# A seven-product (Strassen) block form for the input projection of one hybrid encoder layer

## The chip, the cores and the metric

One core of a Trainium2 chip runs the whole layer in one launch. The metric is the device time of an execution in microseconds, the median of several runs. Its engines are TensorE (PE for its matmuls, PEld for its weight loads), VectorE (DVE), ScalarE (ACT), GpSimd (POOL) and the queue that issues DMAs (SP).

## The reference

One layer, sequence 1024, model width 1024, all in float32:

```python
proj = x @ w_in + b_in                    # [1024, 1024] @ [1024, 8192]
a_u, a_v, a_g, b_z, b_g, c_val, c_glu, c_g, merge, ple_g = split(proj)   # 512 each; merge 3072, ple_g 1024
y_a = gelu(a_u) * spatial_mix(layer_norm(gelu(a_v))) * silu(a_g)
y_b = real(fft2(b_z)) * silu(b_g)
y_c = silu(group_norm(conv31(c_val * sigmoid(c_glu)))) * silu(c_g)
merged = sum(sigmoid(merge[b]) * (y[b] @ w_p[b]) for b in (a, b, c))
out = layer_norm(alpha * x + merged @ w_out + b_out + sigmoid(ple_g) * (p @ w_ple))
```

The input projection is the bulk: 64 output tiles of 128 channels.

## The kernel before, in words

Every float32 operand of a matmul is held as two parts, hi (rounded, a cast on ScalarE) and lo (the rest, a subtraction on VectorE; both in `split`, lines 79 to 81), and each product takes three matmuls: hi with hi, hi with lo, lo with hi. All matmuls that matter have a 128 x 128 stationary operand and 512 moving columns.

x stays in SBUF transposed and split, eight k tiles of 128 rows (`xs`). The projection is walked in units. A channel-major unit (`t_unit`, line 228) computes 128 channels for 1024 positions: 8 k x 3 x 2 halves = 48 matmuls into two PSUM banks, and then an activation or a product takes the banks away. A position-major pass (`natural_pass`, line 145) computes 512 channels with the positions on the partitions: 8 k x 8 position tiles x 3 = 192 matmuls into eight banks; there are four, for b_z, a_v and the two halves of ple_g. Weights come in tiles of 128 x 1024 (512 KB) by `load_split` (line 88): a raw tile by a DMA on SP's queue, then the split; three buffers each of raw, hi and lo, and the whole is put 300 instructions ahead of its place.

The order is written out by hand: b_z, the transform with b's gates, branch B's merges, the spatial gating, branch A's merges with the convolution's normalisation in steps between them, branch C, the embedding product with ple_g, and the output projection with the layer norm. A merge (`merge_pair`, line 325) computes its sigmoid gate by a unit and multiplies it at once with y @ w_p; nothing is written to DRAM but the result. The convolution's 31 taps are 1024-wide VectorE operations (`tap`, line 382) taken from a list, `bgq`, some after each unit. Each engine works its instructions off in order. The tile framework orders them by priority when it builds the program, assigns buffers, and sets the waits for data, for buffers and for banks.

Of the kernel before, what the change touches and what calls it, by code (L numbers as in the profile page):

```python
# [9 lines left out]
F32 = mybir.dt.float32  # L10
# [13 lines left out]
HALF = 512  # L24
AHEAD4 = 60
AHEAD = 300  # instructions by which a weight's split goes ahead of the arithmetic
# [6 lines left out]
R_BZ, R_AV, R_AG, R_AB, R_PG, R_BO, R_LG, R_LB = 0, 512, 1024, 1536, 2048, 3072, 4096, 5120  # L33


@with_exitstack
def hybrid_layer(
# [22 lines left out]
    rows = ctx.enter_context(tc.tile_pool(name="rows", bufs=1))  # L60
    s2 = ctx.enter_context(tc.tile_pool(name="s2", bufs=7))
    xp = ctx.enter_context(tc.tile_pool(name="xp", bufs=16))
    s4 = ctx.enter_context(tc.tile_pool(name="s4", bufs=21))
    st = ctx.enter_context(tc.tile_pool(name="st", bufs=8))
    psp = ctx.enter_context(tc.tile_pool(name="psp", bufs=8, space=bass.MemoryType.PSUM))
# [4 lines left out]
    def slot(shape, dt=F32, name="t4"):  # L70
        return s4.tile([P, *shape], dt, name=name, tag="s4")

    def xslot(name):
        return xp.tile([P, 1024], F32R, name=name, tag="xp")

    def tmp(dt=F32, name="t2"):
        return s2.tile([P, HALF], dt, name=name, tag="s2")

# [4 lines left out]
    def load(src):  # L83
        raw = wraw.tile([P, 1024], F32, name="raw", tag="raw")
        nc.sync.dma_start(out=raw, in_=src)
        return raw

    def load_split(src):
        with tc.high_priority(AHEAD):
            raw = load(src)  # L90
            hi = whi.tile([P, 1024], F32R, name="hi", tag="hi")
            lo = wlo.tile([P, 1024], F32R, name="lo", tag="lo")
            split(hi, lo, raw)
        return hi, lo

    def load_split4(src):
        with tc.high_priority(AHEAD4):
            raw = load(src)
            hi, lo = slot([1024], F32R, "h4"), slot([1024], F32R, "l4")
            split(hi, lo, raw)  # L100
        return hi, lo
# [6 lines left out]
    def row_tile():  # L108
        return rows.tile([P, 1024], F32, name="row", tag="row")

    def mm3(ps, s, m, first, last):
        (sh, sl), (mh, ml) = s, m
        nc.tensor.matmul(ps, lhsT=sh, rhs=mh, start=first, stop=False)  # L113
        nc.tensor.matmul(ps, lhsT=sh, rhs=ml, start=False, stop=False)  # L114
        nc.tensor.matmul(ps, lhsT=sl, rhs=mh, start=False, stop=last)  # L115
# [4 lines left out]
    # ---------------- b_z, in position-major form; x arrives meanwhile  # L120
    xs = []
    col = const.tile([P, C_END], F32, name="col")
# [10 lines left out]
    bsT = const.tile([P, 4, P], F32, name="bsT")  # L133

    def load_x(kt, parts):
        raw = wraw.tile([P, 1024], F32, name="raw", tag="raw")
        hi, lo = xslot("xh"), xslot("xl")
        xs.append((hi, lo))
        n = 1024 // parts
        return [  # L140
            (raw[:, i * n:(i + 1) * n], xT[kt][:, i * n:(i + 1) * n], hi[:, i * n:(i + 1) * n], lo[:, i * n:(i + 1) * n])
            for i in range(parts)
        ]

    def natural_pass(unit, evac, ns=range(NPT), before=None, after=None):
        banks = {n: bank() for n in ns}
        w = None
        for kt in range(KT):
            if before is not None:
                w = before(kt, w)  # L150
            elif kt % 2 == 0:
                w = load_split(w_in[unit + kt // 2])
            wk = sub(w, slice(None), slice((kt % 2) * HALF, (kt % 2 + 1) * HALF))
            for n in ns:
                mm3(banks[n], sub(xs[kt], slice(None), slice(n * P, (n + 1) * P)), wk, kt == 0, kt == KT - 1)
            if after is not None:
                after(kt)
        for n in ns:
            evac(n, banks[n])

    def x_arrives(kt, w):
        if kt == 0:
            raw = wraw.tile([P, 1024], F32, name="raw", tag="raw")
            hi = whi.tile([P, 1024], F32R, name="hi", tag="hi")
            lo = wlo.tile([P, 1024], F32R, name="lo", tag="lo")
            pieces = load_x(0, 2)
            wp = [(raw[:, i * HALF:(i + 1) * HALF], w_in[BZ][:, i * HALF:(i + 1) * HALF],
                   hi[:, i * HALF:(i + 1) * HALF], lo[:, i * HALF:(i + 1) * HALF]) for i in range(2)]
            for r, src, h, l in (wp[0], pieces[0], pieces[1], wp[1]):
                nc.sync.dma_start(out=r, in_=src)  # L170
                split(h, l, r)
            return hi, lo
        for r, src, h, l in load_x(kt, 1):
            nc.sync.dma_start(out=r, in_=src)
            split(h, l, r)
        if kt % 2 == 0:
            w = load_split(w_in[BZ + kt // 2])
        if kt >= KT - 3:
            tab.append(load_split4(tabs[kt - KT + 3]))
        if kt == 1:  # L180
            nc.sync.dma_start(out=col, in_=colp)
            x_arrives.bz = row(tmp(name="row"), R_BZ)
        return w

    tab = []
    zj = [slot([2, HALF], F32, "z") for _ in range(4)]

    def evac_z(n, ps):
        nc.vector.tensor_tensor(out=zj[n // 2][:, n % 2], in0=ps, in1=x_arrives.bz, op=ALU.add)

    natural_pass(BZ, evac_z, before=x_arrives)

    for i in range(2):
        nc.vector.tensor_copy(out=cen[:, i], in_=tab[2][0][:, 768 + i * P:768 + (i + 1) * P].bitcast(F32))
# [6 lines left out]
    def add(o, a, b):  # L201
        nc.vector.tensor_tensor(out=o, in0=a, in1=b, op=ALU.add)

    def subt(o, a, b):
        nc.vector.tensor_tensor(out=o, in0=a, in1=b, op=ALU.subtract)

    def mul(o, a, b):
        nc.vector.tensor_tensor(out=o, in0=a, in1=b, op=ALU.mult)

    s02, s13 = slot([2, HALF], F32, "s02"), slot([2, HALF], F32, "s13")  # L210
    add(s02, zj[0], zj[2])
    subt(zj[0], zj[0], zj[2])
    add(s13, zj[1], zj[3])
    subt(zj[1], zj[1], zj[3])
    add(zj[2], s02, s13)
    subt(zj[3], s02, s13)

    # ---------------- channel-major unit: 128 channels of the projection
    bgq = []

    pace = [0]

    def bg():
        """Some of the instructions that wait to be mixed in."""
        for _ in range(min(pace[0], len(bgq))):
            bgq.pop(0)()

    def t_unit(ct, evac):
        w = load_split(w_in[ct])
        banks = [bank() for _ in range(2)]  # L230
        (wh, wl) = w
        for kt in range(KT):
            ks = slice(kt * P, (kt + 1) * P)
            xh, xl = xs[kt]
            for wt, xt, f, l in ((wh, xh, True, False), (wh, xl, False, False), (wl, xh, False, True)):
                for hf in range(2):
                    nc.tensor.matmul(  # L237
                        banks[hf], lhsT=wt[:, ks], rhs=xt[:, hf * HALF:(hf + 1) * HALF],
                        start=f and kt == 0, stop=l and kt == KT - 1,
                    )  # L240
        for hf in range(2):
            evac(hf, banks[hf])
        bg()

    def act_unit(ct, func, dst):
        def evac(hf, ps):
            nc.scalar.activation(out=dst(hf), in_=ps, func=func, bias=col[:, ct:ct + 1])
        t_unit(ct, evac)

    # ---------------- Fourier mixing  # L250
    gT = [None] * 4
# [4 lines left out]
    def split_group(g):  # L256
        gs = slice(g * P, (g + 1) * P)
        fh, fl = slot([4, 2, P], F32R, "fh"), slot([4, 2, P], F32R, "fl")
        for k in range(4):
            split(fh[:, k], fl[:, k], zj[k][:, :, gs])  # L260
        F[g] = (fh, fl)
# [63 lines left out]
    def merge_pair(branch, y, d2, step=None):  # L325
        wp = load_split(w_p[branch * 4 + d2])
        for i in range(2):
            d = 2 * d2 + i
            if branch == 1:
                merged[d] = slot([1024], F32, "mg")  # L330
# [421 lines left out]
```

## Time and profile before

| | us |
|---|---|
| three runs | 995.39, 995.79, 995.84 |
| median | 995.79 |
| span of the profiled execution | 994.7 |
| TensorE busy | 984.7 (4420 matmuls) |
| VectorE busy | 569.7 |
| ScalarE busy | 294.5 |
| GpSimd busy | 21.2 |
| DMA, mean over the span | 67 GB/s |

Busy time is time with at least one instruction in the engine; matmuls overlap, so a matmul's price is read from the distance between starts in the chain. The granted clock is given as a share of TensorE's full 2.4 GHz; it was 0.999 in the mean.

### The profile page before, as it was taken

What the parts mean: (1) busy time and instruction counts of PE and PEld (TensorE: products, weight loads), DVE (VectorE), ACT (ScalarE), POOL (GpSimd) and SP (SyncE); (2) the same over time, 40 slices, a digit from 0 to 9 for tenths busy, and PEclk for the clock granted to TensorE, in tenths of its full rate; (3) what the DMA queues carried; (4) which work ended last, traced back from release to release, by engine and by line L of the source; (5) the groups of instructions that cost most, each with busy time, mean ns of one, the idle gap of its engine ahead of it and who ended that gap; (6) DMA issues with size and microseconds to landing.
All of it is one profiled execution on the core that took longest, in us unless ns stands there. A gap on an engine that the chain in (4) does not pass through costs nothing.

```text
span 994.7 us, 10596 instructions
## 1 busy us (share of the span) xinstructions
PE 984.7 (99%) x4420; PEld 814.6 (82%) x4420; DVE 569.7 (57%) x684; ACT 294.5 (30%) x424; POOL 21.2 (2%) x20
## 2 busy tenths in 40 slices
PE   9999999999999999999999999999999999999997
PEld 6888888888888888888888888888887888888886
DVE  4553369818979976973445646433231311757587
ACT  4333322121211345233336455332211230333100
POOL 0000000000000210000000000000000000000022
PEclk9999999999999999999999999999999999999999
DMA  8611101111121231111111111111221110232312
GB/s 253 216 43 43 33 31 43 43 64 43 43 74 48 102 106 43 43 46 61 43 43 43 43 64 36 50 43 49 78 64 43 57 60 32 70 112 95 128 64 105
DMA packets 20751, 67.10 MB, mean 67 GB/s; under 512 B 2272, under 2 KB 3168, under 8 KB 20704
## 3 DMA queue, kind: packets, MB, share of 16 engines
q1 hardware_dynamic: 20704, 66.43, 19.8%
q8 instruction: 34, 0.56, 0.2%
q14 instruction: 13, 0.11, 0.0%
HBM read 62.23 MB, written 4.19 MB: 67 GB/s over the span
## 4 chain that ended last, share of the span: by engine, by line
PE 98%; DMA 1%; DVE 0%; ACT 0%; SPq 0%; POOLq 0%; issue 0%
PE ps L237 53%; PE ps L341 13%; PE ps L115 11%; PE ps L114 10%; PE ps L113 10%; DMA raw<-in_xT_dram 1%; PE ps L536 0%; PE ps L537 0%; PE ps L548 0%; PE ps L549 0%; SPq L170 0%; DVE zacc L445 0%; DVE xl L81 0%; ACT xh L80 0%; ACT hi L80 0%; POOLq L748 0%
## 5 line engine op out<-in xcount | busy, mean ns | idle before, releaser
L81 DVE TENSOR_TENSOR lo<-raw,hi 128x1024 fp32r<-128x1024 f32 (+1 forms) x88 | 106.2, 1207 | 236.6 <-ACT hi L80 236.4
L237 PE MATMUL ps<-xh,hi 128*128 128x512 f32 x768 | 236.9, 390 | 0.7 <-ACT hi L80 0.7
L237 PE MATMUL ps<-xl,hi 128*128 128x512 f32 x768 | 236.6, 389 | 0.0
L237 PE MATMUL ps<-xh,lo 128*128 128x512 f32 x768 | 236.5, 389 | 0.0
L80 ACT CAST hi<-raw 128x1024 fp32r<-128x1024 f32 (+1 forms) x88 | 91.9, 1044 | 485.8 <-PE ps L237 341.9
L237 PEld LDWEIGHTS ps<-xh,lo 128*128 128x128 f32 x768 | 144.2, 188 | 30.1
L237 PEld LDWEIGHTS ps<-xl,hi 128*128 128x128 f32 x768 | 144.1, 188 | 30.1
L237 PEld LDWEIGHTS ps<-xh,hi 128*128 128x128 f32 x768 | 143.6, 188 | 30.3 <-ACT hi L80 1.1
L389 DVE SCALAR_TENSOR_TENSOR acc<-h,col,acc 128x1009 f32<-128x1009 f32 (+14 forms) x120 | 153.1, 1276 | 3.3
L113 PE MATMUL ps<-hi,xh 128*128 128x512 f32 x256 | 100.1, 391 | 0.2 <-ACT xh L80 0.2
L115 PE MATMUL ps<-hi,xl 128*128 128x512 f32 x256 | 99.6, 390 | 0.5 <-DVE xl L81 0.5
L114 PE MATMUL ps<-lo,xh 128*128 128x512 f32 x256 | 99.6, 389 | 0.0
L341 PE MATMUL ps<-yh,hi 128*128 128x512 f32 x192 | 59.1, 389 | 0.0
L341 PE MATMUL ps<-yh,lo 128*128 128x512 f32 x192 | 59.1, 389 | 0.0
L341 PE MATMUL ps<-yl,hi 128*128 128x512 f32 x192 | 59.1, 389 | 0.0
L113 PEld LDWEIGHTS ps<-hi,xh 128*128 128x128 f32 x256 | 48.2, 188 | 11.4 <-ACT xh L80 1.4
L115 PEld LDWEIGHTS ps<-hi,xl 128*128 128x128 f32 x256 | 48.0, 188 | 11.0 <-DVE xl L81 1.0
L114 PEld LDWEIGHTS ps<-lo,xh 128*128 128x128 f32 x256 | 48.2, 188 | 9.9
L341 PEld LDWEIGHTS ps<-yh,hi 128*128 128x128 f32 x192 | 36.0, 188 | 7.5
L341 PEld LDWEIGHTS ps<-yl,hi 128*128 128x128 f32 x192 | 36.0, 188 | 7.5
L341 PEld LDWEIGHTS ps<-yh,lo 128*128 128x128 f32 x192 | 36.0, 188 | 7.5
L439 POOL TENSOR_TENSOR rstd<-var,mhalf 128x1 f32<-128x1 f32 x16 | 21.0, 1316 | 968.3 <-DVE var L437 968.3
(134 smaller groups left out, 967.9 us busy)
## 6 DMA issues: line engine op xcount, KB each, us to landing
raw<-in_w_in_dram SPq DMA_DIRECT2D x67, 512.0 KB, 3.3
raw<-in_w_p_dram SPq DMA_DIRECT2D x12, 512.0 KB, 3.2
raw<-in_x_dram SPq DMA_DIRECT2D x16, 256.0 KB, 2.7
raw<-in_w_out_dram SPq DMA_DIRECT2D x8, 512.0 KB, 3.6
raw<-in_xT_dram SPq DMA_DIRECT2D x7, 512.0 KB, 4.9
out_dram<-zacc SPq DMA_DIRECT2D x7, 512.0 KB, 2.6
row<-in_rowp_dram SPq DMA_DIRECT2D x5, 512.0 KB, 5.6
raw<-in_tabs_dram SPq DMA_DIRECT2D x3, 512.0 KB, 3.3
```

Of the source, the lines that this page charges most:

```text
L80: nc.scalar.copy(out=hi, in_=src)
L81: nc.vector.tensor_tensor(out=lo, in0=src, in1=hi.bitcast(F32), op=ALU.subtract)
L113: nc.tensor.matmul(ps, lhsT=sh, rhs=mh, start=first, stop=False)
L114: nc.tensor.matmul(ps, lhsT=sh, rhs=ml, start=False, stop=False)
L115: nc.tensor.matmul(ps, lhsT=sl, rhs=mh, start=False, stop=last)
L237: nc.tensor.matmul(banks[hf], lhsT=wt[:, ks], rhs=xt[:, hf * HALF:(hf + 1) * HALF], start=f and kt == 0, stop=l and kt == KT - 1,)
L341: nc.tensor.matmul(banks[hf], lhsT=wp[wi][:, ws], rhs=y[k][hf][yi], start=f and k == 0, stop=l and k == 3,)
L389: nc.vector.scalar_tensor_tensor(out=acc[i][:, a:b], in0=h[:, a + o:b + o], scalar=w, in1=acc[i][:, a:b], op0=ALU.mult, op1=ALU.add)
L439: nc.gpsimd.tensor_tensor(out=r2, in0=r, in1=mhalf, op=ALU.pow)
```

## The change

The projection is computed in blocks. x is cut into 2 x 2 blocks by halves of the model width and of the positions, and the weights by halves of the width and by two neighbouring units (or two neighbouring 512-channel passes). Seven products of blocks, P1 to P7, give what eight gave. The seven x sides are blocks or sums of blocks, made once and split, and stay in SBUF in place of x (`quad_first`, `quad_rest`). The weight sides that are sums are made by DMAs on GpSimd's queue that add a block of DRAM to the raw tile that holds the previous sum (`plus`). P6 and P7 are added in PSUM to the bank x of P1, P4 and P3 to the banks x and z; copies of the bank are taken in between (`keep`, `kept`).

Units go in pairs (24 of them), two pairs interleaved: P1 of the pair, P7 of the pair before, P2, P4 and P3 of the pair before, P5, P6. A product has 12 matmuls in one bank, and one background step (a mixing tile, a tap, a step of the convolution's normalisation) follows each. The two position-major units (b_z with a_v, the two halves of ple_g) have 4 k x 4 position tiles x 3 matmuls in each product.

Since the x sides fill SBUF, results are not kept: gates, z, v, mixed values, y and the residual are stored to DRAM (`store`) and loaded again. The order becomes: embedding product, b_z with a_v, ple_g, the pairs, then the merges of A, C and B with the transform's steps between them, and the output projection. Raw, hi and lo tiles become 128 x 512, with 9, 6 and 6 buffers; temporary tiles go from 7 to 12.

```diff
-    wraw = ctx.enter_context(tc.tile_pool(name="wraw", bufs=3))
-    whi = ctx.enter_context(tc.tile_pool(name="whi", bufs=3))
-    wlo = ctx.enter_context(tc.tile_pool(name="wlo", bufs=3))
+    rawp = ctx.enter_context(tc.tile_pool(name="rawp", bufs=9))
+    hip = ctx.enter_context(tc.tile_pool(name="hip", bufs=6))
+    lop = ctx.enter_context(tc.tile_pool(name="lop", bufs=6))
...
+    def plus(dst, src):
+        nc.gpsimd.dma_start(out=dst, in_=src, accum_op=ALU.add)
...
+        def product(p, banks, first):            # natural_unit: position-major
+            ws = sides(p)
+            for k in range(4):
+                between(p, k)
+                for n in range(4):
+                    xs = sub(X[p][k], slice(None), slice(n * P, (n + 1) * P))
+                    mm3(banks[n], xs, ws[k], first and k == 0, k == 3, not first)
...
+        product(P6, bx, False)
+        kept("u2", (row1, 1))
+        product(P7, bx, False)
+        kept("u3", (row2, -1))
...
+    def quad_rest(k):
+        b11, b12 = x_block(k, 0, 0), x_block(k, 0, 1)
+        t1 = rawt()
+        subt(t1, b11, b12)
+        split(*X[P5][k], t1)
+        b22 = x_block(k, 1, 1)
+        split(*X[P3][k], b22)
+        subt(b12, b22, b12)
+        split(*X[P7][k], b12)
+        t2 = b11
+        nc.vector.scalar_tensor_tensor(out=t2, in0=t1, scalar=-1.0, in1=b22, op0=ALU.mult, op1=ALU.subtract)
+        split(*X[P6][k], t2)
+        b21 = x_block(k, 1, 0)
+        t4 = t1
+        nc.vector.scalar_tensor_tensor(out=t4, in0=t2, scalar=-1.0, in1=b21, op0=ALU.mult, op1=ALU.subtract)
+        split(*X[P4][k], t4)
...
+        def side(self, p):                       # Pair: channel-major
+            with tc.high_priority(AHEAD):
+                if p == P1:
+                    self.a11, self.a12 = load(self.block(0, 0)), load(self.block(0, 1))
+                    self.a21, self.a22 = load(self.block(1, 0)), load(self.block(1, 1))
+                    return split_w(self.a11)
+                if p == P2:
+                    return split_w(self.a12)
+                if p == P4:
+                    return split_w(self.a22)
+                if p == P7:
+                    plus(self.a11, self.block(1, 0))
+                    return split_w(self.a11)
+                plus(self.a21, {P5: self.block(1, 1), P6: self.block(0, 0), P3: self.block(0, 1)}[p])
+                return split_w(self.a21)
+
+        def product(self, p, b, first):
+            wh, wl = self.side(p)
+            for k in range(4):
+                ks = slice(k * P, (k + 1) * P)
+                mm3(b, (wh[:, ks], wl[:, ks]), X[p][k], first and k == 0, k == 3, not first)
+            bg()
+
+        def keep(self, name):
+            t = tmp(name=name)
+            nc.scalar.copy(out=t, in_=self.x)
+            return t
...
+            elif p == P7:
+                self.product(P7, self.x, False)
+                u3 = self.keep("u3")
+                add(u3, self.z, u3)
+                self.sink[1](1, u3)
+            elif p == P4:
+                self.product(P4, self.x, False)
+                self.sink[1](0, self.x)
+            elif p == P3:
+                self.product(P3, self.z, False)
+                add(self.u2, self.z, self.u2)
+                self.sink[0](1, self.u2)
...
+    for i in range(4):
+        makers += [lambda i=i: c_pair(i), *others[4 * i:4 * i + 4]]
+    makers += others[16:]
+    def run_pairs(makers):
+        prev = None
+        for make in [*makers, None]:
+            cur = make() if make else None
+            for pair, p in ((cur, P1), (prev, P7), (cur, P2), (prev, P4), (prev, P3), (cur, P5), (cur, P6)):
+                if pair is not None:
+                    pair.steps(p)
+            prev = cur
...
+    for d in range(KT):
+        merge_one(0, yA, d, True, step if d > 2 else None)
+    yC = [load_y(d_y["c"][j], AHEAD, nc.gpsimd) for j in range(4)]
+    for d in range(KT):
+        merge_one(2, yC, d, False, step)
+    while steps:
+        step()
+    for d in range(KT):
+        merge_one(1, yB, d, False)
```

`others` begins with a gate pair of C, the four A pairs and the second gate pair of C; then come B's gates and the merge gates.

## Rows read from the trace of the kernel before

**Rows 1.** The page, part 1: busy us, share of the span, instructions.
```profile
span 994.7 us, 10596 instructions
...
PE 984.7 (99%) x4420; PEld 814.6 (82%) x4420; DVE 569.7 (57%) x684; ACT 294.5 (30%) x424; POOL 21.2 (2%) x20
```

**Rows 2.** Chain of waits, 140 to 260 us: start, us, what.
```profile
149.92 5.44 PE ps L341 x24
155.36 10.88 PE ps L237 x48
```

**Rows 3.** Groups by line: busy us, mean ns, then idle before and releaser.
```profile
L237 PE MATMUL ps<-xh,hi 128*128 128x512 f32 x768 | 236.9, 390 | 0.7 <-ACT hi L80 0.7
```

**Rows 4.** Waits of all engines: us in total, times, longest.
```profile
ACT hi L80 <- PE ps L237: 341.9, 44, 14.1
...
PE ps L237 <- ACT hi L80: 0.7, 1, 0.7
```

**Rows 5.** Timeline of SP's queue and TensorE: start, us, what.
```profile
0.73 0.38 SPq L170 DMA_DIRECT2D raw<-in_w_in_dram  x1
...
5.00 0.77 PE L113 MATMUL ps<-hi,xh 128*128 128x512 f32 x1 [0.22 <-ACT xh L80]
...
987.00 0.28 PE L115 MATMUL ps<-h,ml 128*128 128x256 f32 x1
```

**Rows 6.** Groups by line and shape, VectorE and ScalarE.
```profile
L320 ACT ACTIVATE gate<-ps,col 128x512 f32<-128x512 f32 x48 | 30.3, 681 | 0.1
L552 DVE RECIPROCAL sd<-sd 128x512 f32<-128x512 f32 x8 | 26.8, 3352 | 22.1 <-ACT sd L551 22.1
...
L81 DVE TENSOR_TENSOR yl<-g,yh 128x512 fp32r<-128x512 f32 x16 | 10.3, 688 | 0.6
...
L202 DVE TENSOR_TENSOR zacc<-ps,zacc 128x512 f32<-128x512 f32 x15 | 10.0, 685 | 10.1 <-PE ps L115 10.1
...
L80 ACT CAST yh<-g 128x512 fp32r<-128x512 f32 x16 | 9.8, 622 | 4.8 <-DVE g L208 4.8
L81 DVE TENSOR_TENSOR ml<-mg,mh 128x1024 fp32r<-128x1024 f32 x8 | 9.8, 1220 | 7.3 <-ACT mh L80 7.3
...
L599 ACT COPY zacc<-ps 128x512 f32<-128x512 f32 x16 | 9.3, 588 | 9.9 <-PE ps L115 9.9
...
L551 ACT ACT_TABLE_LOAD x7 | 9.0, 1283 | 0.1
...
L371 DVE SCALAR_TENSOR_TENSOR h<-ps,col,sig 128x512 f32<-128x512 f32 x8 | 5.6, 746 | 26.0 <-PE ps L237 26.0
...
L386 DVE TENSOR_SCALAR acc<-h,col 128x1024 f32<-128x1024 f32 x4 | 3.2, 808 | 0.0
...
L389 DVE SCALAR_TENSOR_TENSOR acc<-h,col,acc x120: 1260/1276/1286, 148.1 to 438.2; 128x1009 f32<-128x1009 f32 x8, 128x1010 f32<-128x1010 f32 x8, 128x1011 f32<-128x1011 f32 x8, 128x1012 f32<-128x1012 f32 x8
```

**Rows 7.** Windows at the start: us, busy by engine, clock, DMA share, GB/s.
```profile
0.00:25.00 25.00, 23.06 (x91) 16.63 (x92) 11.43 (x14) 11.13 (x12) 0.20 (x4) 1.00 0.81 253
25.00:50.00 25.00, 25.00 (x112) 20.71 (x111) 14.83 (x18) 8.41 (x8) 0.00 (x0) 1.00 0.64 213
```

**Rows 8.** Windows among the convolution's taps.
```profile
245.00:270.00 25.00, 25.00 (x112) 20.71 (x111) 24.49 (x21) 4.09 (x5) 0.00 (x0) 1.00 0.14 43
...
395.00:420.00 25.00, 25.00 (x112) 20.70 (x111) 24.68 (x25) 5.83 (x7) 0.00 (x0) 1.00 0.19 63
```

**Rows 9.** DMA issues: count, KB each, median us to landing.
```profile
raw<-in_x_dram SPq DMA_DIRECT2D x16, 256.0 KB, 2.7
...
row<-in_rowp_dram SPq DMA_DIRECT2D x5, 512.0 KB, 5.6
...
col<-in_colp_dram SPq DMA_DIRECT2D x1, 100.0 KB, 7.1
```

**Rows 10.** DMA of the whole span.
```profile
DMA packets 20751, 67.10 MB, mean 67 GB/s; under 512 B 2272, under 2 KB 3168, under 8 KB 20704
```

**Rows 11.** Groups by line and shape, the transform's second stage.
```profile
L205 DVE TENSOR_TENSOR yT<-ps,q 128x256 f32<-128x256 f32 x8 | 4.3, 617 | 2.5 <-ACT q L296 2.5
```

More of the change, by code (lines that the diff above doesn't have):

```diff
@@ L161, in x_arrives @@
[L161 to L194, printed above, removed]
+    col = const.tile([P, C_END], F32, name="col")
+    part1 = ExitStack()
+    xq = part1.enter_context(tc.tile_pool(name="xq", bufs=1))
@@ new lines, in hybrid_layer, with x_block, ple_pass @@
+    nc.sync.dma_start(out=col, in_=colp)
+    def x_block(k, half, hf):
+        return load(xT[half * 4 + k][:, hf * HALF:(hf + 1) * HALF])
+    def ple_pass(hf):
+        for n in range(NPT):
+            b = bank()
+            for k in range(2):
+                mm3(b, sub(pts[k], slice(None), slice(n * P, (n + 1) * P)), wpl[hf, k], k == 0, k == 1)
+            t = tmp(name="zp")
+            nc.scalar.copy(out=t, in_=b)
+            store(d_ple[n][hf], t)
+    def plus(dst, src):
+        nc.gpsimd.dma_start(out=dst, in_=src, accum_op=ALU.add)
@@ L195, in hybrid_layer @@
+    ple_pass(0)
+    for k in range(4):
+        quad_first(k, P1, 0, 0)
+    ple_pass(1)
+    rows1 = row(big([1024], name="row"), R_BZ)
+    rows2 = row(big([1024], name="row"), R_AG)
+    wsr = [load(wsT[:, h * HALF:(h + 1) * HALF]) for h in range(2)]
+    wsp = (big([1024], F32R, "wsh"), big([1024], F32R, "wsl"))
+    for h in range(2):
+        split(wsp[0][:, h * HALF:(h + 1) * HALF], wsp[1][:, h * HALF:(h + 1) * HALF], wsr[h])
     for h in range(2):
@@ L216, in hybrid_layer, with mean_rstd @@
[L216 removed]
+    ctab = [load(tabs[2][:, 512:1024])]
+    for i in range(2):
+        nc.vector.tensor_copy(out=cen[:, i], in_=ctab[0][:, 256 + i * P:256 + (i + 1) * P])
+    def mean_rstd(s):
+        mv = st.tile([P, 2], F32, name="mv", tag="mv")
+        nc.vector.bn_aggr(out=mv, in_=s.rearrange("p a b -> p (a b)"))
+        r = st.tile([P, 1], F32, name="var", tag="var")
+        nc.vector.tensor_scalar(r, mv[:, 1:2], EPS, None, op0=ALU.add)
+        r2 = st.tile([P, 1], F32, name="rstd", tag="rstd")
+        nc.gpsimd.tensor_tensor(out=r2, in0=r, in1=mhalf, op=ALU.pow)
+        return mv[:, 0:1], r2
@@ new lines, in affine, with mix_v @@
+    def affine(v, mu, r, g, b):
+        nc.vector.scalar_tensor_tensor(out=v, in0=v, scalar=mu, in1=g, op0=ALU.subtract, op1=ALU.mult)
+        nc.vector.scalar_tensor_tensor(out=v, in0=v, scalar=r, in1=b, op0=ALU.mult, op1=ALU.add)
+    mixq = []
+    ready = []
+    def mix_v(n):
+        vs = tmp(F32R, "vh"), tmp(F32R, "vl")
+        with tc.high_priority(AHEAD4):
+            raw = load(d_v[n])
+        split(*vs, raw)
+        ready.append((n, vs))
+        if len(ready) > 1:
+            mix_mms(*ready.pop(0))
@@ new lines, in hybrid_layer, with slot, load_y @@
+    part1.close()
+    s4 = ctx.enter_context(tc.tile_pool(name="s4", bufs=28, reuse_waits="tile"))
+    def slot(shape, dt=F32, name="t4"):
+        return s4.tile([P, *shape], dt, name=name, tag="s4")
+    merged = [None] * KT
+    def load_y(halves, ahead, queue):
+        pair = slot([1024], F32R, "yh"), slot([1024], F32R, "yl")
+        with tc.high_priority(ahead):
+            for hf in range(2):
+                hs = slice(hf * HALF, (hf + 1) * HALF)
+                raw = pair[1][:, hs].bitcast(F32)
+                queue.dma_start(out=raw, in_=halves[hf])
+                split(pair[0][:, hs], pair[1][:, hs], raw)
+        return [sub(pair, slice(None), slice(hf * HALF, (hf + 1) * HALF)) for hf in range(2)]
@@ new lines, in merge_one @@
+    def merge_one(branch, y, d, first, step=None):
+        ws = load_split(w_p[branch * 4 + d // 2][:, (d % 2) * HALF:(d % 2 + 1) * HALF])
+        banks = [bank() for _ in range(2)]
+        gate = []
+        with tc.high_priority(AHEAD4):
+            for hf in range(2):
+                gate.append(tmp(name="gate"))
+                nc.sync.dma_start(out=gate[hf], in_=d_gate[branch][d][hf])
+        for k in range(4):
+            ks = slice(k * P, (k + 1) * P)
+            for hf in range(2):
+                mm3(banks[hf], sub(ws, slice(None), ks), y[k][hf], k == 0, k == 3)
+        if first:
+            merged[d] = slot([1024], F32, "mg")
+        for hf in range(2):
+            dst = merged[d][:, hf * HALF:(hf + 1) * HALF]
+            if first:
+                mul(dst, banks[hf], gate[hf])
+            else:
+                mul(gate[hf], banks[hf], gate[hf])
+                add(dst, dst, gate[hf])
+        if step is not None:
+            step()
@@ L570, in step @@
+        yB[g] = [sub(pair, slice(None), slice(hf * HALF, (hf + 1) * HALF)) for hf in range(2)]
+    yA = [load_y(d_y["a"][j], AHEAD, nc.gpsimd) for j in range(4)]
+    steps = [load_tabs, lambda: group(0), lambda: None]
+    for g in range(4):
+        steps += [lambda g=g: (stage1(g), group(g + 1) if g < 3 else None), lambda: None, lambda g=g: stage2(g)]
     def step():
-        while bgq:
-            bgq.pop(0)()
         if steps:
             steps.pop(0)()
-    for d2 in range(4):
-        merge_pair(0, yA, d2, step)
```

726 lines of the change are left out of this document (360 added, 366 removed).

## The prediction

> **What bounds the kernel now.** I read the page's busy times first, then the chain of waits, then the groups by line, then the windows, and last the DMA issues. TensorE is busy 984.7 us of a 994.7 us span [rows 1]; VectorE 57%, ScalarE 30%. The chain of waits is made of matmuls almost alone; in it 48 matmuls of 512 columns take 10.88 us and 24 take 5.44 us [rows 2], so one costs 10.88/48 = 0.2267 us from start to start (the 390 ns that a group gives [rows 3] overlap and are no price). The waits table has TensorE waiting less than a microsecond for a weight's split, and ScalarE waiting 341.9 us for TensorE [rows 4]. So a matmul that goes is worth its whole 0.2267 us, as long as VectorE and ScalarE keep in front. Around the span's matmuls lie 5.0 us before the first and 7.4 us after the last's end (987.28) [rows 5]; the runs' median, 995.8 us, is 1.1 us above the profiled span, and I carry that 1.1 over.
>
> **What it removes.** 24 pairs of 128-channel units cost 2 x 48 = 96 matmuls and now 7 products x 4 k x 3 = 84; the two position-major units cost 2 x 192 = 384 and now 7 x 4 x 4 x 3 = 336. Together 24 x 12 + 2 x 48 = 384 matmuls, 384 x 0.2267 = 87.0 us. All other matmuls stay (merges, transform, mixing, embedding, output). The floor is 994.7 - 87.0 = 907.7 us of span. No transposes and no new TensorE work pay for it; everything it costs lies in other engines and in waits.
>
> **The start.** The embedding product comes first. Its first group of matmuls needs four 256 KB pieces where one x piece and one weight piece did; the later of them is the fifth issue on SP's queue (0.38 us each [rows 5]), and the casts behind it run one after another. 3 us (0 to 8).
>
> **The sums of x.** P5's last k needs `quad_rest` of k = 3. VectorE has 30 us for it from P1's start (two products of 48 x 0.2267 = 10.9 us and three quarters of the third). Its work up to there, at 0.688 us for a 512-wide subtraction and 0.685 for a 512-wide addition [rows 6]: P2's four x splits and four weight splits 5.5, the four `kept` 2.7, three whole `quad_rest` of 5 splits and 4 sums 3 x 6.2 = 18.6, the fourth's first sum and split 1.4, P2's four additions 2.7, P5's weight splits 2.8, the mixing weights' 1.4: 35.1 us. About 5 us late, and in the first 60 us some 18 MB move (embedding 2, its spill 4, x 6, weights 4, rows and tables 2), 300 GB/s, against the 253 and 213 GB/s that the first two windows show at a DMA share of 0.81 and 0.64 [rows 7], so loads will not run ahead of it. I take 6 us; ends 0 and 20.
>
> **Bank reuse in the position-major units.** P7 writes the banks that `kept` has just read. Bank 0 is complete three groups (9 matmuls, 2.0 us) before the product ends, and each read takes 0.685, as long as a group of three matmuls; VectorE stays in front if it is not behind for other reasons. 1 us (0 to 8).
>
> **The pairs, the largest term.** Five pairs take 5 x 84 x 0.2267 = 95.2 us of TensorE. VectorE's work in such a block (one convolution pair and four others, one background step a product): 30 taps of 1.276 and the middle one of 0.808, 39.1; the convolution's ending, two reciprocals of 3.35 and eight 512-wide operations, 12.1; its two GLU products 1.5; 35 weight splits of 0.688, 24.1; 15 additions of z, y and kept copies, 10.3 [rows 6]. That is 87.1 us. Each A pair adds four products, 2.7: three A pairs lie in the first block, 95.3 us, one in the second, 89.8, none in the third and fourth, 87.1 each. Before, windows with 24.5 and 24.7 us of VectorE in 25 left TensorE at 25.00 [rows 8]: a full VectorE is no loss by itself. But it queues in order, and P6's weight sum is made by an accumulating DMA on the same buffer as P5's, so it can begin only when P5's split (ScalarE 0.622, VectorE 0.688 [rows 6]) has read it, and P6's cast waits for it to land. Behind that cast stand on ScalarE the copies `u2`, `u3` and the activations, on VectorE the subtraction, the tap and the additions. The six hi/lo buffers let P6's split begin one product, 12 x 0.2267 = 2.72 us, after P5's. So VectorE idles d = 0.62 + 0.69 + L - 2.72 a pair, L from the wait for P5's split to the landing. No row shows an accumulating DMA or one issued by GpSimd. Nearest: 2.7 us for a plain 256 KB load from SP; far: 5.6 us for a broadcast row and 7.1 us for the small column table [rows 9]; from below, L so short that d is 0, with a lag that the taps fill. I take L = 3.4, near the plain load with something for GpSimd's queue and the second read: d = 2. A block then loses what its VectorE work plus 5 d has over 95.2: 10.1, 4.6, 1.9 and 1.9, together 18.5 us. At d = 0 it is 0.1; at L = 5.6 (d = 4.2) it is 62; at L = 7.1 (d = 5.7) 92. The four pairs outside the blocks have no taps and room. ScalarE's own work in a block is less: 35 casts of 0.622, 15 copies of 0.588, 20 activations of 0.68, some 15 table loads of 1.283 and the ending's 7.5, 72 of 95 us; I cost it at nothing, covered by the six buffers' lead of 13.6 us (if not, the third rival below).
>
> The rule of the Trainium skill that bears on L: "DMA: Bandwidth & Descriptors", section "Anatomy of one DMA — SWDGE (gpsimd) path", fits a DMA issued by GpSimd with 2.0 us and the bytes over 436 GB/s; for 256 KB that is an estimate of 2.6 us, d = 1.2, 6.7 us in place of 18.5, and the sum would be 935. It is for a copy, not for an accumulation, and no row here shows either.
>
> **Spills and loads.** Some 36 MB are written to DRAM and read again, and each weight block that enters a sum is fetched once more: 173 MB in place of 67 [rows 10], 183 GB/s over 945 us, under what the first window moved. In a pair it is 3.1 MB in 19 us, 165 GB/s. SP issues about ten DMAs a pair, 0.38 us each, 4 us of 19; a store there waits for its activation and holds up the loads behind it, but these are issued a pair ahead. Nothing for the pairs (already in L), 0 to 10 in the range.
>
> **Merges and transform.** The transform now lies between merges. In the first 16 merges (16 x 5.44 = 87 us and 22 us of transform on TensorE, 109) VectorE has 11 of weight splits, 11 of y splits, 33 of products and additions, 4 of table splits and 4 x 10.7 of transform, 102 us: 93%, 3 us lost to queueing. The last group's stage 2 stands directly in front of branch B: copy 0.59, four larger VectorE operations of up to 0.62 [rows 11] and three small ones, product and split 2.0, about 5 us, of which three quarters of a merge, 4.1, can cover some: 4 us. The first y loads wait for x's last products to free their room: 2 us. Together 9 (0 to 25).
>
> **Output.** The eight merged tiles' splits were under the embedding pass; now they follow the merges, 1.22 us each on VectorE [rows 6] while a k of the output takes 24 x 0.2267 = 5.4. Only the first can be late: 1 us (0 to 8). The tail is as before.
>
> **Sum.** 907.7 + 3 + 6 + 1 + 18.5 + 9 + 1 = 946.2 us of span, with 1.1: **947 us**.
>
> **The rivals.**
> *Nearly the whole gain.* The schedule's lag hides the accumulations (d near 0) and the other waits halve: 907.7 + 10 + 3 + 1.1 = 922. For it: VectorE at 98% cost nothing before, and ScalarE was early by 341.9 us. Against: before, no split waited on a split.
> *Slower.* The accumulating DMA is slow, L like the 7.1 us row. Then 907.7 + 20 + 92 + 1.1 = 1021. The place is the cast of P6's weights in each pair; it decides from where the blocks lose 87 - 20 = 67 us, at d = 4.4, L = 5.8. For it: read, add and write on a busy queue, three in a row on one buffer. Against: it is twice the plain load's 2.7.
> *ScalarE holds the banks.* P4 writes the bank that the copy `u3` reads, and has 2.72 us for it. With a table load of 1.283 and two activations of 0.68 [rows 6] ahead of the copy (0.588), behind P6's cast, it is about 1.5 us late in each pair: 24 x 1.5 = 36 more, 983.
>
> **How the numbers follow.** Forecast (926 to 975) 0.60, nearly whole gain 0.14, slow accumulation 0.16, ScalarE and the banks 0.10, of which 0.01 ends within 0.2% of before and 0.09 faster. 0.2% is about what a measurement of this kernel can tell from no change. So faster 0.60 + 0.14 + 0.09 = 0.83, same 0.01, slower 0.16. The range leaves out half of the first rival and most of the second: 921 to 1000; its upper end takes L = 5.6 with the other terms (907.7 + 20 + 62 + 1.1 = 991) and something of them.
>
> **What would show it.** 4036 matmuls in the page in place of 4420, at 0.227 from start to start. In the pairs: the landing time of the accumulating DMAs, ScalarE's wait of its cast for them, and TensorE's idle time put down to the split or to the copy; VectorE at nine tenths or more there. A first idle stretch near 50 us at P5 for the x split. If TensorE is idle less than 20 us in all, the first rival holds; if the clock's row falls below 1.00 in the pairs, or TensorE's idle time lies at the merges instead, I was wrong about the place.

## The result and the profile after

The changed kernel takes 1050.2 us (1048.9 to 1054.5), the kernel before 995.8 beside it: 1.055 times as long, interval 1.053 to 1.057. The forecast of 947 us and its range up to 1000 were wrong, and so was the sign. The profiled execution took 1054.45 us, with a span of 1052.7.

The page of the changed kernel, part 1, as in [rows 1]:

```profile
span 1052.7 us, 11880 instructions
...
PE 957.0 (91%) x4036; PEld 760.8 (72%) x4036; DVE 704.7 (67%) x1000; ACT 425.2 (40%) x681; POOL 138.9 (13%) x164
```

The matmuls are 4036, as they should be. But TensorE, 99% busy before, is at 91%. Part 2 of the page has the clock, the share of the DMA engines and GB/s in 40 slices:

```profile
PEclk9798998989999999999999998999999899899999
DMA  8988398299755655765756656674674543423012
GB/s 280 308 218 226 130 235 206 100 303 225 189 123 126 156 138 136 174 152 139 179 138 174 172 136 182 159 186 124 202 260 160 200 141 122 170 80 119 1 60 100
```

The first ten slices, 260 us, have the DMA engines near full most of the time; the clock falls in many slices. The whole span's DMA beside [rows 10], the issues beside [rows 9], which have 2.7 us for a plain 256 KB load (count, KB each, median us to landing):

```profile
DMA packets 99709, 174.44 MB, mean 166 GB/s; under 512 B 10816, under 2 KB 19904, under 8 KB 99648
...
raw<-in_w_in_dram SPq DMA_DIRECT2D x128, 256.0 KB, 4.0
raw<-in_w_in_dram POOLq DMA_DIRECT2D x104, 256.0 KB, 4.9
...
a<-in_w_in_dram POOLq DMA_DIRECT2D x24, 256.0 KB, 6.6
```

The two lines with POOLq are the accumulating DMAs, 4.9 and 6.6 us; plain loads take longer too, 4.0 for a weight tile and 3.5 for the x tiles that had 2.7. Waits of all engines, beside [rows 4] (line 88 is the cast, 89 the subtraction, 114 to 116 the three matmuls, 203 the accumulating DMA, 454 the copy of a bank):

```profile
POOL raw L203 <- DVE lo L89: 318.5, 57, 15.5
...
DVE lo L89 <- ACT hi L88: 177.0, 95, 8.2
ACT hi L88 <- DMA raw<-in_w_in_dram: 141.5, 42, 8.3
...
PE ps L114 <- ACT u L454: 22.8, 12, 4.7
...
PE ps L114 <- ACT hi L88: 20.7, 5, 11.2
```

Read upwards it is a ring. TensorE waits for a cast 20.7 us, 11.2 of them once at the start, and twelve times for ScalarE's bank copy `u`, 22.8 us; ScalarE's casts wait for weight tiles' DMAs, sums among them; VectorE's subtractions wait for the casts, and GpSimd's sums wait for the subtractions. One instance, from the timeline in the pairs:

```profile
330.37 0.69 DVE L89 TENSOR_TENSOR lo<-raw,hi 128x512 fp32r<-128x512 f32 x1
...
331.35 0.87 POOL L203 DMA_DIRECT2D raw<-in_w_in_dram  x1 [11.94 <-DVE lo L89]
...
333.95 0.87 POOL L203 DMA_DIRECT2D raw<-in_w_in_dram  x1 [1.73 <-DMA raw<-in_w_in_dram]
...
337.86 1.14 ACT L88 CAST hi<-raw 128x512 fp32r<-128x512 f32 x2 [6.19 <-DMA raw<-in_w_in_dram]
...
338.90 0.58 ACT L454 COPY u<-ps 128x512 f32<-128x512 f32 x1
...
339.54 0.80 PE L114 MATMUL ps<-t,hi 128*128 128x512 f32 x1 [2.89 <-ACT u L454]
```

P5's split of one pair ends at 331.06 and releases the sum for P6, which lands at 337.78; P6's cast on ScalarE starts at 337.86, 6.8 us after the split's end. The copy stands behind the cast. The bank that it reads, P7's of the pair before, was complete at 333.8 (that product's last matmul starts at 333.45, and one takes 0.39); P4, which writes it again, waits until 339.54. Its first matmul then takes 0.80 us, at half clock.

The same can be followed in all 24 pairs by counting casts and products. From the end of P5's split to the landing of P6's sum it takes 3.9 to 9.2 us, 4.3 in median and 4.9 in the mean of the 20 pairs in blocks, and in 21 of the 24 pairs P6's cast starts within 0.1 us of the landing.

To see where the whole time went I took the starts of neighbouring matmuls and subtracted 0.2267 us (0.120 for 256 columns). What is over is counted as *price* where it is under 20 ns outside stretches of granted clock 0.5, as *half clock* up to one more matmul time inside such stretches, and as *wait* else. Before, all of it is 6.7 us. After, it is 98.9 wait, 29.1 half clock and 23.5 price, 151.5. Span: 907.7 - 6.7 + 151.5 = 1052.5, for 1052.7. By stage, wait and half clock together, and for all runs of the block form (a wait at the border of two stages is counted in the one that ends; the losses are those of the profiled execution, which for the changed kernel is the slowest of its four):

| | start | unit 1 | unit 2 | pairs | merges | price | median us |
|---|---|---|---|---|---|---|---|
| forecast | 3 | 7 | 0 | 18.5 | 9 | 0 | 947 |
| after | 15.0 | 15.8 | 19.3 | 50.6 | 26.9 | 23.5 | 1050.2 |
| e1_no_sums | 15.7 | 4.1 | 6.7 | 12.5 | 29.2 | 24.2 | 995.8 |
| e2_no_ple_spill | 3.6 | 12.0 | 19.3 | 52.2 | 28.0 | 23.4 | 1041.4 |
| e3_p5_p6_apart | 15.5 | 15.7 | 19.0 | 22.6 | 27.5 | 23.9 | 1027.1 |
| e4_pool_add | 15.4 | 24.2 | 20.1 | 118.9 | 28.9 | 23.0 | 1133.8 |
| e5_ple_store_act | 3.7 | 25.2 | 19.4 | 50.4 | 27.1 | 23.3 | 1052.1 |
| e6_merge_room | 14.9 | 17.0 | 19.3 | 52.5 | 14.5 | 23.6 | 1044.7 |
| e7_split_pool | 17.2 | 12.8 | 19.3 | 78.7 | 27.0 | 23.2 | 1081.4 |
| e8_combo | 4.0 | 28.4 | 0.8 | 24.9 | 14.8 | 24.0 | 999.7 |
| e9_x_once | 6.9 | 22.2 | 1.5 | 23.2 | 14.3 | 24.3 | 996.6 |
| e10_apart_no_sums | 14.8 | 6.2 | 5.9 | 13.0 | 28.3 | 24.1 | 995.9 |
| e11_st_first | 17.3 | 15.5 | 21.1 | 55.6 | 26.8 | 2.1 | 1041.4 |
| e12_x_once_st_first | 6.5 | 23.4 | 1.3 | 24.5 | 14.0 | 1.5 | 975.6 |

Unit 1 is b_z with a_v, unit 2 the two halves of ple_g. Runs e1 to e8, e10 and e14 to e16 are single executions, the others medians.

### The profile page after: what moved, and what is told of

Read it like the earlier page. It is cut to its first block, busy times and chain, and to the rows that moved or that the text cites. A ratio compares the mean times of both kernels' runs of the same rounds, so it can differ in the third digit from the quotient of the medians.

```text
span 1052.7 us, 11880 instructions
## 1 busy us (share of the span) xinstructions
PE 957.0 (91%) x4036; PEld 760.8 (72%) x4036; DVE 704.7 (67%) x1000; ACT 425.2 (40%) x681; POOL 138.9 (13%) x164
## 5 line engine op out<-in xcount | busy, mean ns | idle before, releaser
L88 ACT CAST hi<-raw 128x512 fp32r<-128x512 f32 x236 | 143.4, 618 | 316.3 <-DMA raw<-in_w_in_dram 141.5
L89 DVE TENSOR_TENSOR lo<-raw,hi 128x512 fp32r<-128x512 f32 x236 | 160.2, 687 | 164.3 <-ACT hi L88 163.1
L114 PE MATMUL ps<-t,hi 128*128 128x512 f32 x384 | 156.3, 407 | 25.5 <-ACT u L454 22.8
L203 POOL DMA_DIRECT2D raw<-in_w_in_dram x104 | 91.2, 947 | 501.1 <-DVE lo L89 318.5
L116 PE MATMUL ps<-t,lo 128*128 128x512 f32 x384 | 154.6, 403 | 0.0
L115 PE MATMUL ps<-t,hi 128*128 128x512 f32 x384 | 153.8, 400 | 0.0
L114 PE MATMUL ps<-b,hi 128*128 128x512 f32 x288 | 115.6, 401 | 5.4 <-ACT hi L88 5.4
L116 PE MATMUL ps<-b,lo 128*128 128x512 f32 x288 | 115.1, 400 | 0.0
L115 PE MATMUL ps<-b,hi 128*128 128x512 f32 x288 | 114.7, 398 | 0.0
L114 PEld LDWEIGHTS ps<-t,hi 128*128 128x128 f32 x384 | 73.5, 192 | 48.6 <-ACT u L454 29.2
L115 PEld LDWEIGHTS ps<-t,hi 128*128 128x128 f32 x384 | 73.7, 192 | 17.2
L114 PE MATMUL ps<-hi,t 128*128 128x512 f32 x128 | 53.5, 423 | 19.1 <-DVE u L122 11.1
L114 PEld LDWEIGHTS ps<-b,hi 128*128 128x128 f32 x288 | 55.1, 191 | 18.7 <-ACT hi L88 5.8
L115 PEld LDWEIGHTS ps<-b,hi 128*128 128x128 f32 x288 | 55.0, 191 | 13.4
L116 PE MATMUL ps<-hi,t 128*128 128x512 f32 x128 | 52.8, 415 | 0.0
```

Source lines behind the costliest of these rows:

```text
L88: nc.scalar.copy(out=hi, in_=src)
L89: nc.vector.tensor_tensor(out=lo, in0=src, in1=hi.bitcast(F32), op=ALU.subtract)
L203: nc.gpsimd.dma_start(out=dst, in_=src, accum_op=ALU.add)
```

## The experiments

**The sums, and the order of P5 and P6.** e1 drops the accumulating DMAs, so that the weight sums, and 33.6 of the 174.4 MB (the text below says 38), are left out:

```diff
-        nc.gpsimd.dma_start(out=dst, in_=src, accum_op=ALU.add)
+        return
```

> Leaves out the accumulating DMAs altogether: the weight sides of P3, P5, P6 and P7 are single blocks instead of sums, all else stays (so also their splits, copies and products). The changed kernel loses 151 us of TensorE's time to waits and half clock: 33 in the first 120 us, 22 in the second position-major unit, 60 in the pairs, 33 in the merges. Theory A (casts and subtractions of the sums wait for accumulating DMAs and hold up the copies queued behind them): the pairs' loss falls from 60 to 20 us or less, the two units' from 40 to under 20; time 985 to 1000. Theory B (ScalarE's own work, table loads among it, makes the copies late): the pairs keep 45 us or more, only the units gain; time 1025 to 1040. Theory C (bytes moved): 38 MB of 174 are gone, 22%; the gain is where the DMA share was above 0.9, before 260 us, and the pairs (share 0.6) keep theirs; time 1015 to 1030.

995.8 us, no more than the 996.1 of the kernel before: without any sum, the other losses eat the whole gain. The pairs fall from 50.6 to 12.5 and units 1 and 2 from 35.1 to 10.8. TensorE's waits in this kernel, where the copy of the bank had 22.8:

```profile
PE ps L114 <- ACT hi L88: 18.2, 3, 11.4
...
PE ps L114 <- ACT u L454: 2.0, 2, 1.0
```

So ScalarE's own load did not make the bank copies late; bytes went with the sums, though. e3 keeps them all and puts three products between P5 and P6, whose sums are made in the same buffer and which followed each other directly:

```diff
-((cur, P1), (prev, P7), (cur, P2), (prev, P4), (prev, P3), (cur, P5), (cur, P6))
+((cur, P1), (prev, P7), (cur, P5), (prev, P4), (cur, P2), (prev, P3), (cur, P6))
```

> Only the order of the interleaved pairs changes: P1, P7 of the pair before, P5, P4 of the pair before, P2, P3 of the pair before, P6; so four products lie between P5 and P6, whose sums are chained on one buffer, in place of one. Theory A: the casts of P6's sums find it landed, ScalarE's wait for accumulating DMAs in the pairs falls by more than half, and the pairs' loss from 60 to 25 us or less; time 1010 to 1025. Theory B: nothing in ScalarE's work changes; the pairs keep 50 us or more; time 1040 to 1055.

1027.1: the pairs lose 22.6 in place of 50.6, with the same sums and bytes. The waits for the copy go here too:

```profile
PE ps L114 <- ACT u L454: 4.1, 4, 1.4
```

So what stood ahead of the copies, a cast waiting for its sum, made them late. e10 has both edits:

> The changed kernel with P5 and P6 a product apart (as e3_p5_p6_apart) and without the accumulating DMAs, so that the weight sums are left out. In the pairs TensorE lost 52 us in waits with sums, 31 with the order changed, 23 without sums in the old order. If what the new order leaves is all the accumulations' landing, the pairs lose 10 or less here. If it is ScalarE's queue of copies and activations, whatever the weights do, they lose 20 to 23 again. Time: 976 to 985 by the first, 987 to 995 by the second.

995.9, and 13.0 in the pairs: the new order alone costs nothing, and the sums' share in the pairs is 50.6 - 12.5 = 38.1 us in the old order and 22.6 - 13.0 = 9.6 in the new. (The 52, 31 and 23 of the text on record are waits with the price in them, which I had not yet told apart; by that count e10 has 23.8, and 13.4 of it turned out to be price. This is what led to the last group of runs.)

**Other ways to make or use the sums.** e4 adds by GpSimd, from a plain load; e7 lets GpSimd split the summed weights of the pairs:

```diff
-        nc.gpsimd.dma_start(out=dst, in_=src, accum_op=ALU.add)
+        r = load(src)
+        nc.gpsimd.tensor_tensor(out=dst, in0=dst, in1=r, op=ALU.add)
```

> Each accumulating DMA becomes a plain load by SP into a raw buffer and an addition on GpSimd; bytes from DRAM, order and products stay. No row shows GpSimd's 512-wide addition; an estimate from its 1.3 us row for one column is 1.5 to 3 us. Theory A: the wait from P5's split to P6's sum falls from about 5.5 to 2 or 3 us; the pairs' loss falls to 25 us or less and the units' to 25; time 1000 to 1015. Rival: nine raw buffers now hold the added blocks too, loads run less far ahead, and what is won at the sums is lost at the loads: 1040 to 1060. Theory C: as many bytes move, no gain before 260 us.

```diff
+        nc.gpsimd.tensor_copy(out=hi, in_=raw)
+        nc.gpsimd.tensor_tensor(out=lo, in0=raw, in1=hi.bitcast(F32), op=ALU.subtract)
```

> In the pairs alone, the four summed weight sides of each pair are split on GpSimd (cast and subtraction) in place of ScalarE and VectorE; the accumulating DMAs and their chain stay. Theory A1 (the chain is quick enough for TensorE; what hurts is the copies and additions queued behind a cast that waits): waits of TensorE for the copies u2 and u3 go, the pairs' loss falls from 64 to 30 us; span 1015 to 1025. Theory A2 (the sums themselves come too late): TensorE waits for the hi and lo of sums instead, the loss stays at 55 us or more; span 1045 or above. GpSimd's addition took 1.56 us in the run with additions there, so four casts and subtractions and four issues of 0.87 fill 13 to 16 of a pair's 19 us: a third outcome is that GpSimd itself is the bound, above 1080.

1133.8 and 1081.4, both much worse. The groups on GpSimd in e4 and in e7 (busy us, mean ns, then idle before and its releasers; lines of their own kernels, in e7 line 122 is a matmul):

```profile
L204 POOL TENSOR_TENSOR raw<-raw 128x512 f32<-128x512 f32 x104 | 161.4, 1559 | 450.0 <-DMA raw<-in_w_in_dram 296.3 <-DVE lo L89 104.8 <-DMA d_res<-u 21.2
```

```profile
L106 POOL TENSOR_TENSOR lo<-raw,hi 128x512 fp32r<-128x512 f32 x96 | 156.4, 1630 | 7.9
L105 POOL CAST hi<-raw 128x512 fp32r<-128x512 f32 x96 | 102.6, 1068 | 121.4 <-DMA raw<-in_w_in_dram 104.0 <-PE ps L122 17.4
```

In e4 GpSimd waits 296 us for plain loads, which now need a second raw buffer each and come later: the accumulating DMA, slow as it is, was the better choice here. In e7 a split takes 1.07 + 1.63 us in place of ScalarE's 0.62 and VectorE's 0.69, on the engine that also issues the sums. Which wait made most of e7's loss was not followed further.

**The start: bytes or a queue.** e2 leaves the embedding product's 4.2 MB of stores out (what read them again reads x in their place); e5 only moves those stores from SP's queue to ScalarE's:

```diff
-            store(d_ple[n][hf], t)
+            nc.scalar.dma_start(out=d_ple[n][hf], in_=t)     # e5; the line is gone in e2
```

> Leaves out the 16 stores of the embedding product (4.2 MB in the first 30 us); where they were loaded again the same number of bytes is loaded from x. Theory C (the start is bound by bytes): the 11.4 us wait before P1's first matmul at 40 us and the half clock behind it shrink to a third; time 1035 to 1040. Theory A' (the wait is the order of loads and the raw buffers, not bytes): the wait stays within 2 us; time 1048 to 1052.

> Only the 16 stores of the embedding product move, from SP's queue to ScalarE's, right behind the copies that make their data; bytes stay. Leaving them out took the wait before P1's first matmul from 11.4 us to about nothing and 12 us from the time. Theory A' (the stores wait on SP's queue for TensorE's copies, one each 1.4 us, and P1's weight loads stand behind them): the wait goes as it did without the stores; span 1038 to 1042. Theory C (4.2 MB of stores in a saturated start): the wait stays at 9 us or more; span 1048 to 1053.

In the changed kernel the first product waits 11.18 us at 40.56; its weights' loads were issued behind the stores. Both edits take that wait away (start 15.0 to 3.6 and 3.7). But e5 loses 25.2 in unit 1, where after had 15.8, and ends at 1052.1, while e2 keeps 8.8 us. So the queue made the wait at 40.56, and without it unit 1 waits instead. That e2, with fewer bytes, loses 12.0 there points at bytes; it is not shown, since e5's stores also hold ScalarE's queue (two issues take 2.56 us at 18.73) and VectorE, which makes the x sides, is busy 17.47 of 20 us from 60 to 80 in e5. Windows of the changed kernel, beside [rows 7]:

```profile
0.00:25.00 25.00, 22.21 (x87) 15.73 (x87) 8.47 (x15) 15.08 (x25) 0.20 (x4) 1.00 0.83 280
25.00:50.00 25.00, 13.82 (x49) 10.46 (x48) 6.01 (x11) 8.01 (x14) 3.74 (x4) 0.73 0.99 298
75.00:100.00 25.00, 16.04 (x65) 12.46 (x66) 15.61 (x26) 8.79 (x15) 4.41 (x5) 0.94 0.92 246
325.00:350.00 25.00, 22.11 (x89) 17.46 (x89) 21.85 (x29) 16.11 (x22) 3.49 (x4) 0.93 0.54 137
```

A DMA share of 0.99 and 0.92, with TensorE at 13.8 and 16.0 of 25 us; the last line is from the pairs.

**The merges.** e6 puts the transform's tables into tiles that the convolution no longer needs, so that others come free, and begins its steps at the second merge, not the fourth:

> Only the merge stage changes: the three split tables go to the six tiles that the convolution no longer needs, so six of the 28 tiles there are free, and the transform's steps begin two merges earlier. The merge stage loses 31 us now (3.4 at the first y loads, 6 with half clock at C's y loads, 5.6 and 5.8 around the transform's last two groups). Theory M1 (room: C's y loads and the transform's z loads start late because no tile is free): the stage's loss falls to 15 us or less; span 1034 to 1039. Theory M2 (latency of the loads that GpSimd issues, eight in a row, and of z): it stays above 25 us; span 1046 to 1053.

```diff
-            pair = slot([1024], F32R, "tabh"), slot([1024], F32R, "tabl")
+            pair = big([1024], F32R, "tabh"), big([1024], F32R, "tabl")
...
-        merge_one(0, yA, d, True, step if d > 2 else None)
+        merge_one(0, yA, d, True, step if d > 0 else None)
```

1044.7: the merges lose 14.5 in place of 26.9, of which 5.5 us show in the time.

**Together.** e8 has the order of e3, the stores of e5 (and the gates' stores) on ScalarE's queue, e6, and the residual's 4.2 MB of x loads moved from unit 2 to the output:

> Four changes together: P5 and P6 apart (27 us in the run with that alone), the embedding's and the gates' stores on ScalarE's queue (12 us expected for the start, 0 to 10 for the gates), the merge stage's room as in the run beside this one, and the residual (4.2 MB of x loads, 16 operations pairs on VectorE) moved from the second position-major unit to the output stage, where the DMA share is 0.1 to 0.3. If the losses are where the accounts put them they add up: 1052.7 - 27 - 12 - 5 - 15 - 8 = 985, range 975 to 1005; if they hide one another, above 1010.

999.7, in the range but 15 above the sum; unit 1 now loses 28.4. Unit 2 falls from 19.3 to 0.8. Whether bytes made its loss is not shown: the residual took 32 VectorE operations with it (from 210 to 235 us VectorE is busy 24.64 of 25 in the changed kernel), e1 without the sums has 6.7 there, and in e8 the same stage runs at a full DMA share almost without loss:

```profile
140.00:160.00 20.00, 19.46 (x84) 15.38 (x83) 13.64 (x26) 5.75 (x9) 9.28 (x12) 1.00 1.07 260
```

e9 loads each block of x once:

```diff
-    for k in range(4):
-        quad_first(k, P1, 0, 0)
+    quad(0)          # all seven sides of k, x's four blocks loaded once
     ple_pass(1)
+    quad(1)
...
-        if p == P1:
-            quad_first(k, P2, 1, 0)
-        elif p == P2:
-            quad_rest(k)
+        if p == P1 and k < 2:
+            quad(k + 2)
```

> On top of e8_combo: each block of x is loaded once and all seven sides are made from it (x's loads 4.2 MB in place of 6.3), two of the four during the embedding product; the mixing weights, 0.75 MB with their tables, are loaded after the first position-major unit; the mixing tiles' splits go ahead with their loads. In e8_combo the first unit lost 21.7 us in waits and 8.8 at half clock, with the DMA engines nearly full from 40 to 100 us. Theory (the start is bound by bytes): leaving out 4.2 MB of spills gave back 15 us of start and unit in e2_no_ple_spill, 3.6 us per MB, so 2.8 MB less give 10 us, and the first mixing tile's wait of 5 us goes too: 986 us. Rival (the first unit is bound by VectorE's queue of splits and sums, which is no shorter): only the mixing tile's wait goes, 996. Rival (all x sums moved early hold up P1 and P2): the first unit loses over 35 us, 1004 or more.

996.6 (ratio to before 1.0004, 0.9993 to 1.0016). My estimate of 986 missed: unit 1 gave back 6.2 us and the start took 2.9 of them, and the mixing tile's wait stayed (6.3 us, now for its cast). From 40 to 60 us VectorE is busy 16.56 of 20 and TensorE 11.93. The early sums may hold up the splits there; in the same stretch ScalarE's casts also wait 3.9 us for a block of x, so this is not shown.

**The price of a matmul.** After all this, e9's 92 us of losses held 24.3 in no wait at all: 512-column matmuls 233 to 234 ns apart, everywhere but in the second half of the output projection. In the changed code the small statistics tiles (1632 bytes) lie between the weight tiles and the x sides. The other pool between them is a multiple of 2048 bytes, so by the code x sides, y and merged tiles start 1632 bytes (modulo 2048, within a partition) behind the weight tiles; before, all start at the same offset. e11 and e12 move one line:

```diff
+    st = ctx.enter_context(tc.tile_pool(name="st", bufs=8))
     rawp = ctx.enter_context(tc.tile_pool(name="rawp", bufs=9))
...
-    st = ctx.enter_context(tc.tile_pool(name="st", bufs=8))
```

> The changed kernel with one line moved: the pool of small statistics tiles (1632 bytes a partition) is declared ahead of the weight tiles and no longer between them and the x sides, so that all matmul operands start at the same offset modulo 2048 bytes (1600), as in the kernel before (2016). In the changed kernel weight tiles start at 2016 and x sides, merged and y tiles at 1600, and outside waits a 512-column matmul with one operand of each kind takes 233 to 234 ns from start to start in place of 226.7 (3626 intervals, 23.7 us together); the second half of the output projection, whose operands are all at 1600, takes 226.7. Theory (the two offsets): the 233 ns become 227 everywhere, and 15 to 26 us come back: 1024 to 1035. Rival (the 233 ns come from waits, DMA traffic or the order of the instructions): no change, 1049 to 1051.

> e9_x_once with the statistics pool moved in the same way. There 3725 intervals of 512 columns carry 24.4 us over 226.7 ns. Theory (the two offsets): 972 to 982, faster than the kernel before. Rival (not the offsets): 995 to 998.

e13 puts the same pool between weights and x in the kernel before:

> The kernel before with the same pool moved to between the weight tiles and x, so that weight tiles start at 2016 and x, y and merged tiles at 1600 modulo 2048 bytes; nothing else changes. Theory (the two offsets): some 4000 of its 4186 intervals go from 226.7 to 233 to 234 ns, 26 to 30 us: 1021 to 1026. Rival (the 233 ns belong to the changed kernel's waits, traffic or order): 995 to 997.

e13: 1021.7, ratio 1.0254 (1.0237 to 1.0271), with nothing else changed. Its chain, where [rows 2] have 5.44 for 24 and 10.88 for 48:

```profile
152.92 5.60 PE ps L341 x24
158.52 11.20 PE ps L237 x48
```

11.20/48 = 0.2333. In e11 the price fell from 23.5 to 2.1 us, but the median only from 1050.2 to 1041.4, under what I expected: waits and half clock grew from 128 to 136 us, in the pairs most. As I read it, where the next weight is late, a faster matmul waits longer. In e12, with the waits reduced first, the 22.8 us of price came out as 21.0 of time: 975.6, ratio 0.9792 (0.9775 to 0.981). This version beats both kernels:

```profile
span 972.3 us, 11820 instructions
...
PE 919.6 (95%) x4036; PEld 751.0 (77%) x4036; DVE 702.5 (72%) x1000; ACT 415.5 (43%) x674; POOL 137.9 (14%) x164
```

e14 to e16 put an unused tile of 32, 64 and 256 bytes there, in the kernel before:

```diff
+    padp = ctx.enter_context(tc.tile_pool(name="padp", bufs=1))
+    nc.gpsimd.memset(padp.tile([P, 8], F32, name="pad"), 0.0)   # e14; 16 in e15, 64 in e16
```

> The kernel before with an unused tile of 32 bytes a partition between the weight tiles and all later tiles: weight tiles stay at 2016 modulo 2048 bytes, x, y and merged tiles go from 2016 to 0. e13_before_st_between had put 1632 bytes there (25.5 times 64) and matmuls took 7 ns more. If the price comes from a difference that is not a multiple of 64 bytes: 1020 to 1023 us, as there. If only larger differences count (256 bytes and more): 995 to 997.

> The same with 64 bytes: x, y and merged tiles at 32 modulo 2048, weight tiles at 2016. If the price comes from a difference that is not a multiple of 64 bytes: none here, 995 to 997. If from any difference modulo 2048: 1020 to 1023.

> The same with 256 bytes: x, y and merged tiles at 224 modulo 2048. Multiple of 64: 995 to 997. Any difference modulo 512 or more: 1020 to 1023.

1020.3, 1008.4 and 996.4 (before 996.6 beside them). The chains of e15 and e16:

```profile
244.85 10.99 PE ps L239 x48
```

```profile
242.24 10.88 PE ps L239 x48
```

32 bytes cost about as much as 1632, 256 nothing, and 64, against both ideas, half: 10.99/48 = 0.2290 in the channel-major units, and some 6.5 ns a matmul in the position-major passes. What between 64 and 256 bytes is free was not tried, nor what in the chip makes it so.

## Why the prediction was wrong

The removed work was right: 384 matmuls, and span and losses add up on the floor of 907.7. What failed:

- **The pairs: 18.5 forecast, 50.6 measured.** The step that failed is "I take L = 3.4". I had bounded L by 7.1 and chosen near the plain load; measured as the prediction defines it, L is 4.3 in median and 4.9 in the mean over the blocks. The place, P6's cast, was right. The path behind it failed too: I let VectorE's fullness pass the delay on. It came through the bank copies behind the waiting cast, the third rival's place for the slow rival's cause; I had costed the two apart. VectorE is at 21.85 of 25 us from 325 to 350, and at 339.5 of 448 from 232 to 680, not full. The prediction's formula with L = 4.9 gives d = 3.5 and 48 us, near the 50.6, but that is luck: it charges a VectorE with 87 to 95 us of work in 95. (ScalarE's 72 us there adds up to 71.) The Trainium skill's fit that the prediction weighed ("DMA: Bandwidth & Descriptors", "Anatomy of one DMA — SWDGE (gpsimd) path") gave an estimate of 2.6 us for 256 KB; the accumulating DMAs here have medians of 4.9 and 6.6, and the measurement decides.
- **The price of a matmul: 0 forecast, 23.5 measured.** The floor carried 0.2267 us over to kernels with other tiles. No row of before showed it: there all large tiles start at one offset.
- **The start and the two units: 10 forecast, 50.1 measured.** The start has 15.0 (3 forecast), unit 1 15.8 (7) and unit 2 19.3 (0). I put spills and loads at nothing by comparing the mean, 183 GB/s, with the first window's 253; but the bytes crowd at the start, where the changed kernel has a DMA share of 0.99 from 25 to 50 us, and I had counted 300 GB/s for the first 60 us myself. The 11.18 us of the start were loads behind stores on one queue (e5). In the units the sums (e1: 35.1 to 10.8), the stores (e2) and the residual (e8) each take away a part; what of it is bytes and what VectorE's and ScalarE's order stays open.
- **The merges: 9 forecast, 26.9.** VectorE's load was counted, and only 2 us for room: e6 shows that room and earlier steps together are worth 12.4. The other 14.5 were not traced to a cause.
- **Half clock: not in the sum**, 29.1 us, which lie within the stages above. I had named a falling clock as a sign of being wrong, and priced it at zero. It follows the waits: e12 with 55 us of waits has 14.7, e4 with 166 has 42.0.
- The output, 1 forecast, lost nothing.

The excesses over the forecast add up to 32.1 + 23.5 + 12.0 + 8.8 + 19.3 + 17.9 - 1 = 112.6; less the 6.7 that the floor held already, 946.2 + 105.9 = 1052.1 of the span's 1052.7.

## What to carry to other kernels

Ask of each new wait which instructions stand behind it on that engine and whether one of them frees a bank: a cast that waits for a DMA is cheap until a bank copy queues behind it. Check bytes against bandwidth by stage, not over the span, and ask in each what waits: a full DMA share cost nothing in e8's second unit. Keep the operands of matmuls at like offsets when adding small pools between large ones, and remove waits before prices: the same line was worth 9 us with all the waits and 21 with fewer.

## What was not expected of the hardware

- Two operands of a 512-column matmul whose tiles start 32 or 1632 bytes apart modulo 2048 cost 0.2333 us in place of 0.2267, and 256 bytes apart nothing more. 64 bytes apart they cost 0.2290 in the channel-major units and 0.233 in the position-major passes.
- An accumulating DMA of 256 KB from GpSimd's queue took 4.9 us in median for the raw tiles (96 of 104 in the pairs) and 6.6 for `a21` in the units; its issue alone holds GpSimd 0.87 us in median.
- GpSimd takes 1.56 us for a 128x512 float32 addition, 1.63 for a subtraction and 1.07 for a cast.
- In the changed kernel TensorE waited from 29.4 to 40.6 us; its granted clock fell to 0.5, that is 1.2 GHz, at 31.9, and stayed there to 45.6, five microseconds into the next matmuls. So a long wait is paid for twice.
